# Grouped-query attention on one core: Q transposed by DMA instead of on TensorE, and separate banks for the last job's sums

## The chip, the cores and the metric

One Trainium2 chip, one core. The metric is the device time of one launch in microseconds; the median of three runs of the kernel before is 434.11 us (433.84 to 435.28).

## The reference

Grouped-query attention: 32 query heads share 8 key/value heads, so each K and V head serves four Q heads.

```python
batch, seq, n_heads, n_kv_heads, dim = 8, 512, 32, 8, 64      # Q, K, V in float32
K_expanded = np.repeat(K, heads_per_group, axis=2)            # heads_per_group = 4, same for V
scores = np.einsum('bhqd,bhkd->bhqk', Q, K_expanded) * scale  # scale = 1 / sqrt(64)
weights = np.exp(scores - np.max(scores, axis=-1, keepdims=True))
weights = weights / (np.sum(weights, axis=-1, keepdims=True) + 1e-10)
output = np.einsum('bhqk,bhkd->bhqd', weights, V_expanded)    # back to [b, q, h, d], float32
```

## The kernel before

The kernel takes exp without subtracting the row maximum (`fast_path`) and checks at the end that all row sums and the squares of V lie within bounds; a flag decides on the device whether `general_path` has to run instead. With these inputs it does not.

The work is cut into units and jobs. A unit `u` (32 of them, `NU`) is one batch and two K/V heads with their eight Q heads; `b, gp = divmod(u, 4)`. A job `j` (64, `NJOB`) is one K/V head `g` of a unit with its four Q heads, held as two pairs (`NPAIR = 2`), because two heads of 64 fill the 128 partitions. A job has 2 pairs x 4 key chunks = 8 tiles of scores, each 128 keys x (2 heads x 512 queries). TensorE computes the transposed scores (L196), so that the softmax weights come out with keys on the partitions, ready to be the stationary operand of the product with V (L262). V carries a column of ones, so the 65th column of that product is the row sum.

Seven of the eight tiles go through ScalarE: `act_tile` (L207) writes two PSUM banks, one ACTIVATE (L212) takes 128x1024 scores to f16 weights `pt`. The eighth, pair 1 and chunk 0, is computed on VectorE by bit arithmetic in three steps, `exp_d` (L220), `exp_d2` (L228, L231) and `exp_d3` (L238, L239).

The order on each engine is written out by hand in the loop at L359: `tc.manual_schedule()` keeps program order, and each engine works through its own queue with semaphores between them. Job `j`'s scores are interleaved with the weighted sums `pv(last, ...)` and the normalisation `norm(last, ...)` of the job before it, so an extra round `j = NJOB` finishes the last job. `norm` takes a reciprocal of the sums (L287), multiplies (L291) into `o_sb`, and after a unit's last pair issues the unit's store (L328) on SP's queue; the last unit is stored pair by pair. Every 16 reciprocals are checked by two instructions (`in_bounds`, L273); `check_v` (L174, L181) squares V on TensorE.

Q and K must be transposed so that the head dimension lies on the partitions. Loads cast to bf16 and are issued on POOL's queue (`load_q` L123, `load_k` L100, `load_v` L108). K of the first batch is transposed on TensorE (`first_k`); K of later batches by four DMA transposes a batch from SBUF to SBUF on SP's queue (`dma_k` L148), 128 x 512 each, and two copies (L153) that swap the halves. Q is transposed on TensorE: in job `j`, `trans_q(j + 1, ...)` makes eight transposes (L161) into one bank of `d_ps`, and VectorE copies the bank (L164) to `qt`.

PSUM has eight banks: `s_pool` 2 x 2 for ScalarE's tiles, `d_pool` 2 for VectorE's tile, the Q transposes and `check_v`, and `pv_pool` 2 for the weighted sums. `q_nat` has three buffers, so `load_q(u + 2)` at the head of job `2u` waits on POOL for the transposes of unit `u - 1`.

Of the kernel before, what the change touches and what calls it, by code (L numbers as in the profile page):

```python
# [33 lines left out]
VV_HI = 1.0e30  # L34


@with_exitstack
def kernel(
    ctx: ExitStack,
    tc: tile.TileContext,  # L40
    Q: bass.AP,
    K: bass.AP,
    V: bass.AP,
    out: bass.AP,
):
    nc = tc.nc
    flag_pool = ctx.enter_context(tc.tile_pool(name="flag", bufs=1))
    flag = flag_pool.tile([1, 1], I32, name="flag")
    with ExitStack() as fast, tc.manual_schedule():
        fast_path(fast, tc, Q, K, V, out, flag)  # L50
    good = nc.values_load(flag, min_val=0, max_val=128)
    with tc.If(good < 128):
        general_path(tc, Q, K, V, out)


def fast_path(ctx, tc, Q, K, V, out, flag):
# [11 lines left out]
    SPB = 16  # L68

    const_pool = ctx.enter_context(tc.tile_pool(name="const", bufs=1))  # L70
    qnat_pool = ctx.enter_context(tc.tile_pool(name="qnat", bufs=3))
    knat_pool = ctx.enter_context(tc.tile_pool(name="knat", bufs=2))
    qt_pool = ctx.enter_context(tc.tile_pool(name="qt", bufs=3))
    kt_pool = ctx.enter_context(tc.tile_pool(name="kt", bufs=2))
# [80 lines left out]
    def trans_q(j, bank, lo=0, hi=NPAIR):  # L155
        u, g = divmod(j, 2)
        ps = bank.bitcast(BF16).rearrange("p (i sc c) -> p i sc c", i=NPAIR, sc=SC)
        for i in range(lo, hi):
            for sc in range(SC):
                h = g * HPG + 2 * i  # L160
                nc.tensor.transpose(ps[:, i, sc, :], qn[u][:, sc, h:h + 2, :], ident)  # L161
        if j not in qt:
            qt[j] = qt_pool.tile([128, NPAIR, S], BF16, name="qt")
        return lambda: nc.vector.tensor_copy(  # L164
            out=qt[j][:, lo:hi, :], in_=ps[:, lo:hi, :, :].rearrange("p i sc c -> p i (sc c)")
        )


    def check_v(u, bank):
# [16 lines left out]

    NJOB = NU * 2
    DPAIR = NPAIR - 1
    tiles = [(i, kc) for i in range(NPAIR) for kc in range(SC) if (i, kc) != (DPAIR, 0)]
    jobs, osb, invs, ends = {}, {}, {}, []  # L190

    def scores(j, ps, i, kc, m):
# [3 lines left out]
        nc.tensor.matmul(  # L196
            ps,
            keys[64 * m:64 * m + 64, g ^ m, kc * 128:(kc + 1) * 128],
            qt[j][64 * m:64 * m + 64, i, :],
            start=True,  # L200
            stop=True,
        )

    def open_job(j):
        jobs[j] = {"pt": pt_pool.tile([128, NPAIR, SC, 2, S], FP16, name="pt")}

    def act_tile(j, n):  # L207
        i, kc = tiles[n]
        ps = s_pool.tile([128, 2, S], FP32, name="s_ps")
        for m in range(2):  # L210
            scores(j, ps[:, m, :], i, kc, m)
        nc.scalar.activation(out=jobs[j]["pt"][:, i, kc, :, :], in_=ps, func=EXP, scale=scale)  # L212

    def exp_d(j):
        st = jobs[j]
        ps = d_tile()
        for m in range(2):
            scores(j, ps[:, m, :], DPAIR, 0, m)
        st["u"] = dve_pool.tile([128, 2, S], I16, name="u16")
        nc.vector.tensor_scalar(  # L220
            out=st["u"], in0=ps, scalar1=A_U, scalar2=B_U, op0=ALU.mult, op1=ALU.add
        )

    def exp_d2(j):
        st = jobs[j]
        st["f"] = dve_pool.tile([128, 2, S], I16, name="f16")
        st["g"] = dve_pool.tile([128, 2, S], BF16, name="g16")
        nc.vector.tensor_single_scalar(  # L228
            out=st["f"], in_=st["u"], scalar=1023, op=ALU.bitwise_and
        )  # L230
# [3 lines left out]

    def exp_d3(j):
        st = jobs[j]
        w16 = dve_pool.tile([128, 2, S], BF16, name="w16")
        nc.vector.tensor_tensor(out=w16, in0=st["g"], in1=st["f"], op=ALU.mult)  # L238
        nc.vector.tensor_tensor(  # L239
            out=st["pt"][:, DPAIR, 0, :, :].bitcast(U16), in0=st["u"], in1=w16, op=ALU.add  # L240
        )

    def blocks(j):
        kcs = (1, 2, 0, 3) if j == NJOB - 1 else (1, 2, 3, 0)
        return [(kc, m, qc) for kc in kcs for m in range(2) for qc in range(SC)]

    def pv(j, i, lo, hi):
# [2 lines left out]
        b, gp = divmod(u, GP)  # L250
        if lo == 0:

            end = j == NJOB - 1 and i == NPAIR - 1
            pool, name = (s_pool, "s_ps") if end else (pv_pool, "pv")
            t = pool.tile([128, 2, S], FP32, name=name).rearrange(
                "p m (qc c) -> p m qc c", qc=SC
            )
            st["pv"] = t[:, :, :, 0:D + 1]
        order = blocks(j)
        for n in range(lo, hi):  # L260
            kc, m, qc = order[n]
            nc.tensor.matmul(  # L262
                st["pv"][:, m, qc, :],
                st["pt"][:, i, kc, m, qc * 128:(qc + 1) * 128],
                vt[b % 2][:, kc, 2 * gp + g, :],
                start=(n < 2 * SC and qc == 0),
# [3 lines left out]
    def in_bounds(outs, inv, first):  # L270
        ops = ((1.0 / SUM_HI, ALU.is_ge), (1.0 / SUM_LO, ALU.is_le))
        for out_, in1, (bound, op) in zip(outs, (first, outs[0]), ops):
            nc.vector.scalar_tensor_tensor(  # L273
                out=out_, in0=inv, scalar=bound, in1=in1, op0=op, op1=ALU.mult
            )

    def norm(j, i):
        st = jobs[j]
        u, g = divmod(j, 2)
        if u not in osb:  # L280
            osb[u] = osb_pool.tile([128, SC, 2 * HPG, D], FP32, name="o_sb")
        n = j * NPAIR + i
        k, n = divmod(n, SPB) if n < NJOB * NPAIR - 1 else (-1, 0)
        if k not in invs:
            invs[k] = inv_pool.tile([128, SPB, 2, SC], FP32, name="inv")
        inv = invs[k][:, n]
        nc.vector.reciprocal(out=inv, in_=st["pv"][:, :, :, D:D + 1])  # L287
        if k < 0:
            last_check(inv.rearrange("p m qc -> p (m qc)"))
        h = g * HPG + 2 * i  # L290
        nc.vector.tensor_tensor(  # L291
            out=osb[u][:, :, h:h + 2, :].rearrange("p qc m d -> p m qc d"),
            in0=st["pv"][:, :, :, 0:D],
            in1=inv[:, :, :, None].to_broadcast((128, 2, SC, D)),
            op=ALU.mult,
        )
# [1 line left out]
            store(u, h, h + 2)  # L298
        elif g == 1 and i == NPAIR - 1:
            store(u, 0, 2 * HPG)  # L300
        end = j == NJOB - 1 and i == NPAIR - 2
        if k >= 0 and (n == SPB - 1 or end):
            cols = (n + 1) * 2 * SC
            flat = invs.pop(k).rearrange("p s m qc -> p (s m qc)")[:, 0:cols]
            in_bounds((ok[:, 0:cols], ok[:, 0:cols]), flat, ok[:, 0:cols])
        if end:
            vmax = const_pool.tile([128, 1], FP32, name="vmax")
            nc.vector.tensor_reduce(out=vmax, in_=okv, op=ALU.max, axis=AX.X)
            okmin = const_pool.tile([128, 1], FP32, name="okmin")
# [3 lines left out]
            )  # L313


    def last_check(inv):
        cols = 2 * SC
        part = const_pool.tile([128, cols], FP32, name="part")
        right = const_pool.tile([128, cols], BF16, name="right")
        in_bounds((part, right), inv, okall[:, :].to_broadcast((128, cols)))  # L320
        count = d_tile()
        nc.tensor.matmul(count[0:1, 0, 0:cols], ones, right, start=True, stop=True)
        ends.append(count[0:1, 0, 0:cols])

# [31 lines left out]
    trans_q(0, bank[:, 0, :], 0, 1)()  # L356


    for j in range(NJOB + 1):  # L359
        real = j < NJOB  # L360
        last = j - 1
        late = last >= 0
        u, g = divmod(j, 2)
        b, gp = divmod(u, GP)
        if real:
            open_job(j)
            if j == 1:

                nc.gpsimd.tensor_copy(out=gate, in_=jobs[0]["pt"][0:1, 0, SC - 1, 0, 0:1])
                load_q(2)  # L370
            if g == 0 and u >= 1 and u + 2 < NU:
                load_q(u + 2)
            if gp == 1 and b + 1 < B:
                if g == 0:
                    load_k(b + 1)
                else:
                    load_v(b + 1)
            if gp == 2 and g == 0 and b + 1 < B:
                dma_k(b + 1)
            act_tile(j, 0)  # L380
            if j == 0:
                trans_q(0, bank[:, 1, :], 1, NPAIR)()
                act_tile(j, 1)
                exp_d(j)
            else:
                exp_d(j)
                act_tile(j, 1)
        if late:
            pv(last, 0, 0, 11)
        if real:  # L390
            act_tile(j, 2)
            exp_d2(j)
        if late:
            pv(last, 0, 11, 22)
        if real:
            act_tile(j, 3)
        if late:
            pv(last, 0, 22, 32)
            norm(last, 0)
        if real:  # L400
            act_tile(j, 4)

            bank = d_tile()
            reads = []
            if j + 1 < NJOB:
                reads.append(trans_q(j + 1, bank[:, 0, :]))
                if j == 1:
                    for swap in range(2):
                        reads.append(first_k(1, swap, bank[:, 1, swap * S // 2:]))
                elif j > 1 and b == 0 and gp + 1 < GP:  # L410
                    reads.append(first_k(gp + 1, g, bank[:, 1, :]))
            if g == 0 and u > 0:
                reads.append(check_v(u - 1, bank[:, 1, S // 2:]))
            elif j == NJOB - 1:
                reads.append(check_v(u, bank[:, 1, S // 2:]))
            for read in reads:
                read()
            exp_d3(j)
            act_tile(j, 5)
        if late:  # L420
            pv(last, 1, 0, 16)
        if real:
            act_tile(j, 6)
        if late:
            pv(last, 1, 16, 32)
            norm(last, 1)
            del jobs[last]
    nc.vector.tensor_reduce(out=flag, in_=ends[0], op=ALU.min, axis=AX.X)


# [115 lines left out]
```

## Time and profile before

| | |
|---|---|
| median of three runs | 434.11 us |
| the profiled execution, its own time | 435.11 us |
| its span, first to last instruction | 433.4 us |
| granted TensorE clock | 0.996 |
| PE / DVE / ACT busy | 388.4 / 376.7 / 414.4 us |
| first and last ACTIVATE | from 8.98 to 424.65 us |
| DMA moved | 66.97 MB in 91439 packets, mean 155 GB/s |
| q0, loads cast on the way | 25.17 MB, packets' time 49.8% of 16 engines' span |
| q1, stores, copies and transposes | 40.90 MB, 33.1% |

PE is TensorE, DVE VectorE, ACT ScalarE, POOL GpSimd, SP SyncE; SP computes nothing and issues DMAs. "L212" is line 212 of the kernel. In a row of a timeline the numbers are the start and the length of the piece in us, and the bracket at the end is the idle time before it with what ended it. In the DMA row each of 40 digits is the busy share of a slice in tenths. A share of over 1 in a window means that an engine has more than one packet under way.

### The profile page before, as it was taken

The page shows a single profiled execution, that of the slowest core. Times are in us where ns is not written, and L with a number is a line of the kernel's source. Part 1 is how long each engine was busy: PE and PEld are TensorE (multiplying, and loading weights), DVE is VectorE, ACT ScalarE, POOL GpSimd, SP SyncE. Part 2 cuts the span into 40 slices and gives each one's busy share as a digit, 9 for nine tenths or more (in the row PEclk, how much of TensorE's full clock was granted, in tenths as well). Part 3 has the DMA queues.
Part 4 walks back from the last instruction along what each step waited for, and adds up shares of the span by engine and source line. Part 5 has one row for each costly group of instructions (what it writes and reads, how often), then busy time and mean ns, then how long its engine had stood idle before and what let it go on. Part 6 is the DMA issues. An engine that isn't in the chain of part 4 may idle for free.

```text
span 433.4 us, 13542 instructions
## 1 busy us (share of the span) xinstructions
PE 388.4 (90%) x5945; PEld 243.2 (56%) x5945; DVE 376.7 (87%) x704; ACT 414.4 (96%) x449; POOL 63.9 (15%) x89
## 2 busy tenths in 40 slices
PE   7889898999989999899999999999998999999983
PEld 2455555556556556555555555555655655655552
DVE  1698998988999888998889898898899988899884
ACT  2999999999999999999999999999999999999991
POOL 8700004000040001300031000400004000000000
PEclk9999999999999999999999999999999999999998
DMA  9998756987589943998539986699757994352223
GB/s 104 178 141 181 175 151 79 217 149 190 149 128 264 144 130 120 203 210 191 144 74 208 192 192 153 78 216 154 189 149 122 264 173 108 119 146 98 98 95 106
DMA packets 91439, 66.97 MB, mean 155 GB/s; under 512 B 52080, under 2 KB 74608, under 8 KB 91376
## 3 DMA queue, kind: packets, MB, share of 16 engines
q0 software_dynamic: 56544, 25.17, 49.8%
q1 hardware_dynamic: 34832, 40.90, 33.1%
q8 instruction: 47, 0.77, 0.7%
q14 instruction: 16, 0.13, 0.2%
HBM read 50.33 MB, written 33.55 MB: 194 GB/s over the span
## 4 chain that ended last, share of the span: by engine, by line
ACT 39%; DVE 31%; PE 24%; issue 3%; POOL 1%; DVEq 0%; ACTq 0%; POOLq 0%
ACT pt L212 39%; PE s_ps L196 9%; PE pv L262 7%; DVE pt L239 7%; DVE qt L164 7%; DVE w L238 6%; PE d_ps L161 6%; DVE o_sb L291 5%; DVE inv L287 2%; DVE u L220 2%; PE d_ps L174 1%; DVE ok L273 1%; DVE f L228 1%; DVE kt_first L143 1%; POOL q_nat L123 0%
## 5 line engine op out<-in xcount | busy, mean ns | idle before, releaser
L212 ACT ACTIVATE pt<-s_ps 128x1024 f16<-128x1024 f32 x448 | 413.1, 1099 | 9.4 <-PE s_ps L196 9.0
L262 PE MATMUL pv<-v,pt 128*128 128x65 bf16 x4064 | 180.0, 195 | 18.4 <-DVE o_sb L291 18.0
L262 PEld LDWEIGHTS <-pt 128*128 128x128 f16 x4096 | 142.7, 98 | 93.7 <-issue 56.3
L196 PE MATMUL s_ps<-qt,kt 64*128 64x512 bf16 x784 | 153.5, 383 | 16.0 <-ACT pt L212 6.9
L291 DVE TENSOR_TENSOR o_sb<-pv,inv 128x512 f32<-128x512 f32 x127 | 87.8, 692 | 4.4
L196 PEld LDWEIGHTS <-kt 64*128 64x128 bf16 x896 | 54.0, 93 | 55.6 <-issue 25.0
L220 DVE TENSOR_SCALAR u<-d_ps 128x1024 int16<-128x1024 f32 x64 | 77.8, 1215 | 1.4 <-PE d_ps L196 1.4
L123 POOL DMA_DIRECT2D q_nat<-in_Q_dram x34 | 25.4, 748 | 308.0 <-PE d_ps L174 261.3
L164 DVE COPY qt<-d_ps 128x1024 bf16<-128x1024 bf16 (+1 forms) x65 | 44.4, 683 | 16.9 <-PE d_ps L174 11.7
L239 DVE TENSOR_TENSOR pt<-u,w 128x1024 uint16<-128x1024 int16 x64 | 44.3, 693 | 6.5
L238 DVE TENSOR_TENSOR w<-g,f 128x1024 bf16<-128x1024 bf16 x64 | 43.6, 682 | 0.0
L161 PE MATMUL d_ps<-ident,q_nat 128*128 128x128 bf16 x512 | 40.7, 223 | 0.9 <-DVE kt_first L143 0.9
L161 PEld LDWEIGHTS <-q_nat 128*128 128x128 bf16 x512 | 29.3, 99 | 16.2 <-issue 15.1
L287 DVE RECIPROCAL inv<-pv 128x8 f32<-128x8 f32 x127 | 25.8, 204 | 12.5 <-PE pv L262 10.9
L231 DVE TENSOR_SCALAR g<-f 128x1024 bf16<-128x1024 int16 x64 | 29.2, 457 | 2.2
L228 DVE TENSOR_SCALAR f<-u 128x1024 int16<-128x1024 int16 x64 | 27.9, 435 | 2.2
L108 POOL DMA_DIRECT2D v<-in_V_dram x32 | 28.4, 899 | 4.2 <-PE pv L262 2.5
L196 PE MATMUL s_ps<-qt,kt_first 64*128 64x512 bf16 x112 | 24.3, 431 | 1.9 <-ACT pt L212 1.1
L196 PE MATMUL d_ps<-qt,kt 64*128 64x512 bf16 x112 | 21.4, 376 | 0.0
L196 PEld LDWEIGHTS <-kt_first 64*128 64x128 bf16 x128 | 6.9, 96 | 10.3 <-issue 6.7
L174 PE MATMUL d_ps<-v 128*64 128x64 bf16 x256 | 10.6, 201 | 0.0
L174 PEld LDWEIGHTS <-v 128*64 128x64 bf16 x256 | 7.0, 110 | 3.4 <-issue 0.2
(35 smaller groups left out, 44.7 us busy)
## 6 DMA issues: line engine op xcount, KB each, us to landing
out_dram<-o_sb SPq DMA_DIRECT2D x31, 1024.0 KB, 6.2
q_nat<-in_Q_dram POOLq DMA_DIRECT2D x31, 512.0 KB, 6.3
k_nat<-in_K_dram POOLq DMA_DIRECT2D x7, 512.0 KB, 10.8
v<-in_V_dram POOLq DMA_DIRECT2D x28, 128.0 KB, 12.7
kt<-kt SPq DMA_DIRECT2D x14, 256.0 KB, 6.6
out_dram<-o_sb SPq DMA_DIRECT2D x4, 256.0 KB, 2.5
kt<-k_nat SPq DMA_TRANSPOSE x28, 4.7
v<-in_V_dram POOLq DMA_DIRECT2D x4, 96.0 KB, 8.8
```

The costliest lines, as they stand in the source:

```text
L161: nc.tensor.transpose(ps[:, i, sc, :], qn[u][:, sc, h:h + 2, :], ident)
L164: return lambda: nc.vector.tensor_copy(out=qt[j][:, lo:hi, :], in_=ps[:, lo:hi, :, :].rearrange("p i sc c -> p i (sc c)"))
L196: nc.tensor.matmul(ps, keys[64 * m:64 * m + 64, g ^ m, kc * 128:(kc + 1) * 128], qt[j][64 * m:64 * m + 64, i, :], start=True, stop=True,)
L212: nc.scalar.activation(out=jobs[j]["pt"][:, i, kc, :, :], in_=ps, func=EXP, scale=scale)
L220: nc.vector.tensor_scalar(out=st["u"], in0=ps, scalar1=A_U, scalar2=B_U, op0=ALU.mult, op1=ALU.add)
L228: nc.vector.tensor_single_scalar(out=st["f"], in_=st["u"], scalar=1023, op=ALU.bitwise_and)
L231: nc.vector.tensor_scalar(out=st["g"], in0=st["f"], scalar1=-EXP_F1, scalar2=EXP_K, op0=ALU.add, op1=ALU.mult)
L238: nc.vector.tensor_tensor(out=w16, in0=st["g"], in1=st["f"], op=ALU.mult)
L239: nc.vector.tensor_tensor(out=st["pt"][:, DPAIR, 0, :, :].bitcast(U16), in0=st["u"], in1=w16, op=ALU.add)
L262: nc.tensor.matmul(st["pv"][:, m, qc, :], st["pt"][:, i, kc, m, qc * 128:(qc + 1) * 128], vt[b % 2][:, kc, 2 * gp + g, :], start=(n < 2 * ...
L287: nc.vector.reciprocal(out=inv, in_=st["pv"][:, :, :, D:D + 1])
L291: nc.vector.tensor_tensor(out=osb[u][:, :, h:h + 2, :].rearrange("p qc m d -> p m qc d"), in0=st["pv"][:, :, :, 0:D], in1=inv[:, :, :, Non ...
```

## The change

Three edits.

First, Q of units 2 to 31 is no longer transposed on TensorE and copied by VectorE. At the head of job `2u + 1`, `dma_q(u + 2)` issues four DMA transposes on SP's queue from `q_nat` to `qt`, which now holds a whole unit (both heads). `trans_q` stays for units 0 and 1. `q_nat` has four buffers, `load_q` runs three units ahead, and `load_q(3)` is issued with `load_q(2)` in job 1.

Second, the last job's weighted sums no longer use `pv_pool`: pair 0 takes a tile of `d_pool`, pair 1 one of `s_pool`. Half of pair 0's matmuls are issued before the last job's sixth tile, the rest after the job before has been normalised; the extra round of the loop is gone. The order of the key chunks in the sums is changed (2, 3, 1, 0; in the last job 0, 1, 2, 3 and 2, 0, 1, 3).

Third, the last three reciprocals of the kernel, instead of the last one, are checked together at the end (`NLAST`), and the reductions over all earlier checks follow the fourth from last; the last unit's `check_v` moves to the last job but one. The remaining edits generalise VectorE's share of the tiles (`WIDE`, `taken`); with `WIDE` always false VectorE takes the same tile as before.

```diff
+Q_DMA_FROM = 2
+WIDE = lambda j: False
...
-    qnat_pool = ctx.enter_context(tc.tile_pool(name="qnat", bufs=3))
+    qnat_pool = ctx.enter_context(tc.tile_pool(name="qnat", bufs=4))
...
+    def dma_q(u):
+        qt[u] = qt_pool.tile([128, 2, NPAIR, S], BF16, name="qt")
+        for sc in range(SC):
+            nc.sync.dma_start_transpose(
+                out=qt[u][:, :, :, sc * 128:(sc + 1) * 128].rearrange("p g i c -> p (g i) c"),
+                in_=qn[u][:, sc, :, :].rearrange("p h d -> p (h d)"),
+            )
...
-            qt[j][64 * m:64 * m + 64, i, :],
+            qt[u][64 * m:64 * m + 64, g, i, :],
...
-    def blocks(j):
-        kcs = (1, 2, 0, 3) if j == NJOB - 1 else (1, 2, 3, 0)
+    def blocks(j, i):
+        if j == NJOB - 1:
+            kcs = (0, 1, 2, 3) if i == 0 else (2, 0, 1, 3)
+        else:
+            kcs = (2, 3, 1, 0)
...
-            end = j == NJOB - 1 and i == NPAIR - 1
-            pool, name = (s_pool, "s_ps") if end else (pv_pool, "pv")
+            if j < NJOB - 1:
+                t = pv_pool.tile([128, 2, S], FP32, name="pv")
+            else:
+                t = d_tile() if i == 0 else s_pool.tile([128, 2, S], FP32, name="s_ps")
...
+    NLAST = 3
+    inv_last = const_pool.tile([128, NLAST, 2, SC], FP32, name="inv_last")
...
+        p = j * NPAIR + i
+        left = NJOB * NPAIR - p
+        k, n = divmod(p, SPB)
+        if left <= NLAST:
+            inv = inv_last[:, NLAST - left]
...
-    for j in range(NJOB + 1):
+    for j in range(NJOB):
+        end = j == NJOB - 1
...
+            load_q(2)
+            load_q(3)
+        if g == 0 and u >= 1 and u + 3 < NU:
+            load_q(u + 3)
...
+        if g == 1 and Q_DMA_FROM <= u + 2 < NU:
+            dma_q(u + 2)
...
+        if not end:
             bank = d_tile()
...
+            if (j + 1) // 2 < Q_DMA_FROM:
                 reads.append(trans_q(j + 1, bank[:, 0, :]))
...
+            if j == NJOB - 2:
+                reads.append(check_v(u, bank[:, 1, S // 2 + D:]))
...
+        else:
+            pv(j, 0, 0, 16)
+        for read in reads:
+            read()
+        exp_d3(j)
+        act_tile(j, 5)
         if late:
             pv(last, 1, 0, 16)
...
+        if end:
+            pv(j, 0, 16, 32)
+            norm(j, 0)
+            pv(j, 1, 0, 32)
+            norm(j, 1)
```

## The prediction

> **What bounds the kernel now.** I read the page's busy times first, then ScalarE's timeline, the chain of waits at the end, the DMA row with windows of it, and SP's timeline.
>
> The page's busy line:
>
> ```profile
> PE 388.4 (90%) x5945; PEld 243.2 (56%) x5945; DVE 376.7 (87%) x704; ACT 414.4 (96%) x449; POOL 63.9 (15%) x89
> ```
>
> ACT has 448 exponentials of 413.1/448 = 0.922 us and stands at 96%. Its timeline tells where the other 4% is (third column: the idle time before the piece):
>
> ```profile
> 8.98 4.95 ACT L212 ACTIVATE pt<-s_ps 128x1024 f16<-128x1024 f32 x5 [6.81 <-PE s_ps L196]
> ...
> 46.55 29.62 ACT L212 ACTIVATE pt<-s_ps 128x1024 f16<-128x1024 f32 x32 [0.17 <-PE s_ps L196]
> 76.58 348.07 ACT L212 ACTIVATE pt<-s_ps 128x1024 f16<-128x1024 f32 x379 [0.40 <-PE s_ps L196]
> ```
>
> ACT starts at 8.98 us and, from 76.58 on, runs 379 tiles without a gap until 424.65. So nothing that PE or DVE saves between those times can shorten the program: only the 8.98 us ahead, the short waits up to 76.58 and the 8.75 us behind 424.65 are there to be won. The change leaves the number of ACT tiles as it is (`WIDE` is false everywhere). The end, from the chain that ended last:
>
> ```profile
> 424.12 0.70 DVE o_sb L291
> 424.87 1.17 PE pv L262 x32
> 426.07 0.22 DVE inv L287
> 426.31 0.69 DVE o_sb L291
> 427.00 0.20 DVE ok L273
> ...
> 428.55 0.60 DVE o_sb L291
> ```
>
> After ACT's last tile come two rounds of 32 matmuls, reciprocal and product, with the range checks between them; the last product ends at 429.15, and 4.2 us of store and shutdown follow. Beside this stands a resource that is not on the chain, the 16 DMA engines:
>
> ```profile
> DMA  9998756987589943998539986699757994352223
> ```
>
> Slices 6 to 34 of 40 average 0.70: in a batch (eight jobs, 51.4 us) the engines stand idle for some 15 us.
>
> **What goes from PE and DVE.** Jobs 4 to 63 lose 8 transposes and one copy each:
>
> ```profile
> L164 DVE COPY qt<-d_ps 128x1024 bf16<-128x1024 bf16 (+1 forms) x65 | 44.4, 683 | 16.9 <-PE d_ps L174 11.7
> L161 PE MATMUL d_ps<-ident,q_nat 128*128 128x128 bf16 x512 | 40.7, 223 | 0.9 <-DVE kt_first L143 0.9
> ```
>
> 60 x 0.683 = 41.0 us of DVE and 480/512 x 40.7 = 38.2 us of PE. Both lie beside ACT: over a batch (window 77.60 to 129.00) PE is busy 47.25 and DVE 46.45 of 51.4 us, ACT all of it. I cost their saving at nothing but ACT's waits from job 4 on, 0.17 + 0.40 = 0.57 us (bounds 0 and 0.57; the second wait comes where DVE is late with `o_sb`, and 0.68 us less per job covers it). The earlier waits stay, since jobs 1 to 3 keep their transposes. The cover is ACT; were it gone, as much as 0.6 us a job would show.
>
> **The end.** The new order gives the last job's two pairs banks of their own, so their 64 matmuls no longer wait for `o_sb`. In the times of before: the product of job 62's first pair ends at 421.95; now the range checks of that moment follow (427.00 to 428.03 before, with their first 0.08: 1.11 us), less the `check_v` reduction of 0.21; the two products of `exp_d3`, 1.48 us (422.00 to 423.48), end at about 424.4; reciprocal and product of job 62's second pair take 0.93 (425.3), of job 63's first 0.93 (426.3); the last round takes 0.24 + 0.28 (its two checks) + 0.68 = 1.20: 427.5. PE is done earlier: 423.25 after the last scores, 16 + 16 + 32 matmuls of 0.60, 0.60 and 1.17 us: 425.6. So DVE sets the end and the last product comes 1.6 us sooner (429.15 - 427.5). Bounds: 2.7, if DVE's queue did not bind (424.65 + 0.5 + 1.20 = 426.4), and 0.8, if half of it is lost to waits. The moved load of unit 3 and the four `q_nat` buffers touch nothing on this path.
>
> **What is added.** Thirty units get four DMA_TRANSPOSE each, 120, on SP's queue, each 128 x 512 into four blocks, the shape that `dma_k` already issues 28 times. SP's timeline shows its price:
>
> ```profile
> 239.09 0.37 SPq L328 DMA_DIRECT2D out_dram<-o_sb  x1
> 239.56 7.77 SPq L148 DMA_TRANSPOSE kt<-k_nat  x4
> 249.70 1.11 SPq L153 DMA_DIRECT2D kt<-kt  x2
> ```
>
> Four take SP 6.6 to 7.8 us to issue; the copy behind them, which waits for their landing, starts 8.0 to 10.1 us after the first issue (249.70 - 239.56; mean 9.1). `dma_q(u + 2)` is issued right behind store(u - 1), at the start of job 2u + 1, and is first read at job 2u + 4: three jobs, 19.3 us, so a single group leaves 10.2 us. Queued behind it on SP are the next store (12.8 us later) and, once a batch, `dma_k`. There the chain is longest: store 0.45, Q group 6.8, K group up to its copies 9.1, copies 1.1, store 0.45, Q group until landed 9.1 = 27.0 us, against five jobs, 32.1 us. SP alone is in time, by 5.1 us. On POOL the Q load now waits for the landed transposes of four units before instead of PE; K and V loads behind it have over a job to spare.
>
> What decides is the DMA engines' time. Windows cut to the packets of the seven K groups (us, then each engine's busy time, granted clock, DMA share, GB/s):
>
> ```profile
> 36.00:40.50 4.50, 3.85 (x66) 2.26 (x63) 4.26 (x9) 4.40 (x5) 0.00 (x0) 1.00 0.96 128
> 88.80:94.50 5.70, 5.13 (x80) 3.31 (x78) 4.72 (x9) 5.70 (x7) 0.00 (x0) 1.00 0.99 123
> 242.80:249.00 6.20, 5.63 (x89) 3.54 (x85) 5.19 (x11) 6.20 (x8) 0.18 (x1) 1.00 1.44 134
> 346.10:349.80 3.70, 3.23 (x50) 2.00 (x48) 3.49 (x7) 3.70 (x5) 0.00 (x0) 1.00 1.38 215
> sum 35.00, PE 31.14 PEld 19.59 DVE 30.84 ACT 34.90 POOL 0.18; mean PE 4.45 PEld 2.80 DVE 4.41 ACT 4.99 POOL 0.03
> ```
>
> A group holds the engines for 35.0/7 = 5.0 us (3.7 to 6.2) with a share of about 1 or above, though its 0.52 MB would flow in 1.8 us at the 287 GB/s that the best slices of these windows reach:
>
> ```profile
> GB/s 365 355 330 317 302 287 240 165 125 53 60 40 60 60 25 40 35 73 245 292 285 290 120 143 300 287 287 268 23 8 0 40 165 202 222 210 215 198 28 0
> ```
>
> Here, in 140.30 to 144.40, stores run out, the flow falls to 25 to 60 GB/s for 1.1 us while packets are outstanding, then comes back. I read this as transposes holding engines while they wait for a late one. No load is in flight in these windows, so whether loads could use such waits is not shown: the price of a group lies between 1.8 and 6.2 us of engine time. I take the mean, 5.0, as the only rows of this operation.
>
> The room: a batch's other work at full flow (windows where one kind runs alone: loads 202 GB/s, V 159, stores 412, copies 210) is 5 x 2.6 for Q and K, 3.3 for V, 4 x 2.55 for stores, 2.5 for copies, 5.0 for the K group: 34.0, leaving 17.4 us; the DMA row leaves 15.3. Middle: 16.3. Four Q groups ask 20.0. Each batch is short by 3.7 us; six batches have the whole load: 22.2 us, less the lead of 10.2 that must be used up first: 12.0 us of waiting, seen as ACT waiting for scores at the first jobs of a batch.
>
> The K groups move 16 blocks of 128x128 in 5.0 us. A rule of the Trainium skill speaks against the change here: VectorE: DVE Perf Modes, section The three transpose paths, gives 390 ns for such a block on TensorE and 1309 ns on the DMA crossbar, and advises TensorE where PSUM will do. Taken one after another, 16 blocks would be an estimated 20.9 us a unit, over the unit's 12.8, and the kernel some 240 us slower; the row contradicts that. Another page, DMA: Bandwidth & Descriptors, section Queues, rings and completion order, has each engine alternate between rings by packet; if that also holds while a transpose waits, loads fill the waits and the sum is that of the faster rival below.
>
> **The sum.** The profiled execution took 435.11 us, 1.7 around its span of 433.4, and lies 1.0 above the median of 434.1. Against itself: 435.1 - 1.6 - 0.6 + 12.0 = 444.9; on the scale of the median 443.9, which I give as 444. The last term is the weak one. A group at 4.4 gives 17.6 - 16.3 = 1.3 a batch, 7.8 in six, within the lead: nothing. At 6.2, 8.5 a batch: 41 us, 473.
>
> **Rivals.** Hidden (faster): If a group costs at most (16.3 + 10.2/6)/4 = 4.5 us of the engines, the lead is never used up: 434.1 - 2.2 = 431.9, with the tail's bounds 430.8 to 433.3. For it: 5.0 is close to 4.5, the two fastest groups are at 3.7 and 4.1, and part of a group's waits may serve other queues. Against: four of the seven groups take over 5.3 with nothing beside them.
>
> Used up by the waits (no change): Group 5.0, room 17.4: 2.6 short a batch, 15.6 - 10.2 = 5.4; at 4.75 it is 1.6 x 6 - 10.2, nothing. Between these, where waits pay back about 2.2 us, the time stays at 433 to 435.
>
> SP's chain late (slower): If each transpose takes SP the longest seen, 2.34 us, a group takes 9.4, and the chain 27.0 + 3 x 2.6 = 34.8 us against 32.1: 2.7 a batch, seven batches, +19: 451. It decides from 5.1 us of delay on. Against: issue is slow only behind a store that still flows.
>
> **How the numbers follow.** About 0.3%, 1.3 us, can be told from no change. Engines short (the forecast): 0.42, own range 436 to 460; SP's chain 0.08; hidden 0.40; used up 0.10. Faster 0.40, same 0.10, slower 0.50. The range takes in the hidden case from 431.0, and reaches to 460, a group of 5.6 us: (22.4 - 16.3) x 6 - 10.2 = 26.4.
>
> **What would show it.** Right: DMA row at 9 throughout, ACT waiting for PE's scores behind `qt` or `kt` DMAs at jobs 8, 16, 24, Q groups of over 4.5 us. Wrong: ACT in one piece from about 46 us on with the DMA row below 9, transposes landed well over a job ahead. The tail's step is right if the last `o_sb` comes 2.9 us after ACT's end instead of 4.5. The GB/s row at a Q group beside a load tells whether the waits are filled.

## The result and the profile after

The changed kernel takes 465.02 us (median of four runs, 461.19 to 471.34) against 434.00 before (433.84 to 435.28): ratio 1.068, 95% interval 1.0619 to 1.0741. Some runs, one of these four among them, were in a slower state, over 1.5% above the fastest run of their kernel; the ratios, and from here on all times, leave such runs out, which makes the changed kernel 463.28 us. The forecast was 444.0 with a range of 431 to 460. Slower was right, the size was not. The profiled execution of the changed kernel took 463.28 us, 1.7 around its span of 461.6; against the 435.11 of before, 28.2 us more are to be found.

The page: busy times, granted clock and DMA row.

```profile
PE 370.3 (80%) x5465; PEld 226.8 (49%) x5465; DVE 343.4 (74%) x644; ACT 416.2 (90%) x449; POOL 63.5 (14%) x89
PEclk9999999899998999999989999899999799999999
DMA  9999999999999999999899998999999999964314
```

PE has 480 instructions fewer and DVE 60, as the change says (their busy times fell by 18 and 33 us), and ACT fell from 96% to 90% of the span: it now waits. The granted clock, at 9 before in all slices but the last, dips in five slices. The DMA row, 0.70 on average in slices 6 to 34 before, is at 9 almost to the end. ACT's timeline tells where it waits (start, length, tiles, and in the bracket the idle time ahead of the piece):

```profile
8.98 4.95 ACT L236 ACTIVATE pt<-s_ps 128x1024 f16<-128x1024 f32 x5 [6.81 <-PE s_ps L218]
...
82.18 51.89 ACT L236 ACTIVATE pt<-s_ps 128x1024 f16<-128x1024 f32 x56 [2.42 <-PE s_ps L218]
138.06 3.09 ACT L236 ACTIVATE pt<-s_ps 128x1024 f16<-128x1024 f32 x3 [4.00 <-issue]
...
293.22 2.85 ACT L236 ACTIVATE pt<-s_ps 128x1024 f16<-128x1024 f32 x3 [3.13 <-issue]
...
363.83 3.09 ACT L236 ACTIVATE pt<-s_ps 128x1024 f16<-128x1024 f32 x3 [4.16 <-PE s_ps L218]
...
368.36 86.27 ACT L236 ACTIVATE pt<-s_ps 128x1024 f16<-128x1024 f32 x94 [0.18 <-PE s_ps L218]
```

What ran from 46.55 us on with a single wait of 0.40 us is cut at eleven places, each the first tile of a unit. I counted, from the end of one tile to the end of the next, what goes over ACT's pitch of 0.917 us: 34.7 us in all, against 4.7 before. Of the 30.0 more, 27.9 stand at the heads of jobs 6, 8, 10, 18, 24, 26, 32, 34, 40, 42 and 50 (0.6 to 4.3 each), 2.9 in the tiles behind them, and -0.8 before job 6. Less 1.8 us at the end (below) this makes the 28.2. After job 50 nothing waits; the last K and V loads, those of batch 7, are issued at 347 to 356 us, around that job.

What PE waited for, from the list of waits (us in total, times, longest), and from the page's table of DMA issues the median time from issue to landing:

```profile
PE s_ps L218 <- DMA qt<-q_nat: 27.8, 10, 4.2
...
PEld L218 <- DMA qt<-q_nat: 5.2, 3, 2.4
```

```profile
q_nat<-in_Q_dram POOLq DMA_DIRECT2D x31, 512.0 KB, 9.2
...
qt<-q_nat SPq DMA_TRANSPOSE x120, 8.7
...
kt<-k_nat SPq DMA_TRANSPOSE x28, 5.7
```

It is Q's transposes that come late. K's took 4.7 us to land before, and Q's loads 6.3. SP's timeline, from the store of unit 16 (job 35) to the group of unit 21:

```profile
258.48 0.38 SPq L373 DMA_DIRECT2D out_dram<-o_sb  x1
258.96 10.00 SPq L175 DMA_TRANSPOSE qt<-q_nat  x4
269.07 8.18 SPq L152 DMA_TRANSPOSE kt<-k_nat  x4
281.57 1.11 SPq L157 DMA_DIRECT2D kt<-kt  x2
282.78 0.65 SPq L373 DMA_DIRECT2D out_dram<-o_sb  x1
283.54 7.80 SPq L175 DMA_TRANSPOSE qt<-q_nat  x4
291.38 0.58 SPq L373 DMA_DIRECT2D out_dram<-o_sb  x1
292.08 8.47 SPq L175 DMA_TRANSPOSE qt<-q_nat  x4
```

This is the chain that the prediction had at 27.0 us: store, Q group, K group up to its copies, copies, store, Q group. Here the last Q transpose of unit 20 is issued at 291.34, 32.9 us after the store, with its landing still to come, and unit 20 is first read five jobs (32.1 us) after that point. ACT then waits up to 293.22, the start of job 40, the line shown above. Behind it unit 21 is late as well (job 42, 1.8 us). The same distance in each batch, with what the job that reads that group waited:

| store of unit | 0 | 4 | 8 | 12 | 16 | 20 | 24 |
|---|---|---|---|---|---|---|---|
| to the last Q issue of the unit four later, us | 32.5 | 29.9 | 29.3 | 33.3 | 32.9 | 29.4 | 27.9 |
| job that reads it, and its wait, us | 8: 2.6 | 16: 0 | 24: 1.0 | 32: 3.9 | 40: 3.2 | 48: 0 | 56: 0 |

Where the distance passes 32.1 us, the job waits; at 29.9 and below there is little or nothing. The other waits of over 1 us (10, 18, 26, 34, 42, 50) are those of the next group on the queue, the one issued behind this chain. They are the larger part: 16.6 of the 27.9 us, against 10.7 at jobs 8, 24, 32 and 40 and 0.6 at job 6. Those six groups are issued 5.1 to 9.1 us after the head of their job, because the queue is still at work on the chain, and their last transpose lands 15.6 to 17.8 us after the first issue, with the next batch's K and V loads in flight; three jobs hold 19.3 us. Units 29 to 31, issued when no load is left to fly beside them, land in 8.2 to 8.7.

Windows cut to Q groups (each engine's busy time, granted clock, DMA share, GB/s) answer the open question whether loads fill the transposes' waits; the last two show PE around the stall of job 18:

```profile
207.00:211.00 4.00, 3.47 (x54) 2.22 (x53) 3.39 (x8) 4.00 (x5) 0.00 (x0) 1.00 1.44 65
240.00:244.00 4.00, 3.53 (x61) 2.29 (x62) 3.67 (x9) 4.00 (x6) 0.97 (x2) 1.00 1.19 177
253.00:257.00 4.00, 4.00 (x55) 2.24 (x53) 2.65 (x6) 3.81 (x6) 0.00 (x0) 0.66 2.07 141
220.00:222.00 2.00, 1.84 (x32) 1.27 (x31) 1.84 (x3) 2.00 (x3) 0.00 (x0) 1.00 1.20 197
...
216.00:217.00 1.00, 0.41 (x4) 0.11 (x3) 0.97 (x3) 1.00 (x3) 0.00 (x0) 1.00 1.33 255
134.00:138.00 4.00, 0.63 (x4) 0.33 (x6) 0.31 (x1) 0.07 (x1) 0.22 (x1) 0.78 1.64 159
138.00:143.00 5.00, 5.00 (x52) 2.55 (x48) 2.99 (x6) 4.39 (x5) 0.54 (x1) 0.50 1.44 218
```

A load alone (220 to 222) flows at 197 GB/s, transposes alone (216 to 217) at 255; both in flight move 65 to 177 GB/s at a share over 1. Loads do not fill the transposes' waits: the two together move less than either alone.

The end, from the chain that ended last:

```profile
447.85 2.21 ACT pt L236 x2
...
455.25 0.69 DVE o_sb L333
456.50 0.60 DVE o_sb L333
```

ACT's last tile ends at 454.63 and the last product at 457.10, 2.5 us later (4.5 before; 2.9 forecast).

### The profile page after: what moved, and what is told of

Read it like the earlier page. It is cut to its first block, busy times and chain, and to the rows that moved or that the text cites. A ratio compares the mean times of both kernels' runs of the same rounds, so it can differ in the third digit from the quotient of the medians.

```text
span 461.6 us, 12745 instructions
## 1 busy us (share of the span) xinstructions
PE 370.3 (80%) x5465; PEld 226.8 (49%) x5465; DVE 343.4 (74%) x644; ACT 416.2 (90%) x449; POOL 63.5 (14%) x89
## 4 chain that ended last, share of the span: by engine, by line
ACT 40%; PE 20%; DMA 15%; SPq 9%; issue 2%; DVE 1%; ACTq 0%; DVEq 0%
ACT pt L236 40%; DMA qt<-q_nat 15%; PE s_ps L218 10%; PE pv L296 9%; SPq L175 9%; DVE o_sb L333 1%; PE d_ps L218 1%; PE d_ps L186 0%; ACTq L236 0%; DVE pt L265 0%; DVE w L264 0%; DVE ok L307 0%; DVE inv_last L329 0%; DVE okmin L351 0%; DVE inv L329 0%
## 5 line engine op out<-in xcount | busy, mean ns | idle before, releaser
L218 PE MATMUL s_ps<-qt,kt 64*128 64x512 bf16 x784 | 159.9, 398 | 74.4 <-ACT pt L236 32.8
L296 PEld LDWEIGHTS <-pt 128*128 128x128 f16 x4096 | 147.0, 99 | 82.4 <-issue 58.4
L296 PE MATMUL pv<-v,pt 128*128 128x65 bf16 x4032 | 183.7, 197 | 2.4 <-DVE o_sb L333 2.0
L218 PEld LDWEIGHTS <-kt 64*128 64x128 bf16 x896 | 58.7, 94 | 116.7 <-issue 79.7
L333 DVE TENSOR_TENSOR o_sb<-pv,inv 128x512 f32<-128x512 f32 x125 | 86.4, 692 | 4.5 <-DVE inv L329 0.2
L112 POOL DMA_DIRECT2D v<-in_V_dram x32 | 27.9, 885 | 30.6 <-PE pv L296 24.5
L218 PE MATMUL d_ps<-qt,kt 64*128 64x512 bf16 x112 | 22.5, 394 | 0.0
L104 POOL DMA_DIRECT2D k_nat<-in_K_dram x10 | 7.6, 765 | 1.2 <-POOLq L583 0.8
L147 DVE COPY kt_first<-d_ps 128x512 bf16<-128x512 bf16 x8 | 3.2, 418 | 5.2 <-PE d_ps L144 5.1
L193 DVE TENSOR_REDUCE okv<-d_ps 128x1 f32<-128x64 f32 x32 | 6.8, 216 | 0.0
```

Of the source, the lines that this page charges most:

```text
L112: nc.gpsimd.dma_start(out=vt[b % 2][:, sc, lo:hi, 0:D], in_=V[b, sc * 128:(sc + 1) * 128, lo:hi, :],)
L218: nc.tensor.matmul(ps, keys[64 * m:64 * m + 64, g ^ m, kc * 128:(kc + 1) * 128], qt[u][64 * m:64 * m + 64, g, i, :], start=True, stop=True,)
L296: nc.tensor.matmul(st["pv"][i][:, m, qc, :], st["pt"][:, i, kc, m, qc * 128:(qc + 1) * 128], vt[b % 2][:, kc, 2 * gp + g, :], start=(n < 2 ...
L333: nc.vector.tensor_tensor(out=osb[u][:, :, h:h + 2, :].rearrange("p qc m d -> p m qc d"), in0=sums[:, :, :, 0:D], in1=inv[:, :, :, None].t ...
```

## The experiments

Two theories went in. A (A1 and S in the later texts): the DMA engines have too little time in every batch, and lead is a credit that is used up. C (C1 and O): SP's queue, worked off in order, is longer from store to Q group than its five jobs of lead, and nothing is carried on. All kernels start from the changed one; ratios stand to the kernel before on the same chip.

### The two halves of the change

**tail_only**, no unit by DMA:

```diff
-Q_DMA_FROM = 2
+Q_DMA_FROM = 32
```

> The changed kernel with Q of every unit on TensorE again (Q_DMA_FROM = 32); the other edits stay: the last job's banks, the checks of the last three reciprocals, four q_nat buffers, Q loaded three units ahead. Theory A (the DMA engines have too little time once the Q transposes are added) and its rival C (SP's queue issues them too late) both expect the waits to be gone: 434.0 less the 1.77 us that the end of the changed kernel's profile is shorter, 432.3 us. If some other edit made the waits, about 460.

432.64 us, ratio 0.9967 [0.9954, 0.9980] to 434.28: 1.6 us. The last job's banks are worth what the prediction's end step said.

**half_units**, the odd units by DMA:

```diff
+by_dma = lambda u: u >= 2 and u % 2 == 1
...
-        if g == 1 and Q_DMA_FROM <= u + 2 < NU:
+        if g == 1 and u + 2 < NU and by_dma(u + 2):
...
-            if (j + 1) // 2 < Q_DMA_FROM:
+            if not by_dma((j + 1) // 2):
```

> Only every second unit (3, 5, 7 and so on) has its Q transposed by DMA, the others on TensorE. A: two Q groups a batch at about 4.6 us ask 9.2 of the engines' room of 14 us a batch: no waits, 432.3 us, as with all on TensorE. If a Q group cost the engines over 7 us where loads lie beside it, waits stay and it is over 434. C: SP has two groups fewer in each batch and is in time: 432.3 too.

433.37 us, 0.9984 [0.9971, 0.9997], no wait at the head of any unit. Half the transposes cost next to nothing, and win nothing either, as ACT sets the time. Which theory holds is not told by this.

### What makes it slow: bytes, transposes, or loads beside them

**plain_copies**, Q's transposes become plain copies of the same 128 KB (the blocks stay untransposed):

```diff
-            nc.sync.dma_start_transpose(
+            nc.sync.dma_start(
...
-                in_=qn[u][:, sc, :, :].rearrange("p h d -> p (h d)"),
+                in_=qn[u][:, sc, :, :].rearrange("p (k two) d -> p k (two d)", two=2),
```

> The changed kernel with each of the 120 Q transposes replaced by a plain copy of the same 128 KB from the same tile to the same tile (so the scores are of untransposed Q). If the bytes moved inside SBUF were the load, the time stays near 460. A: a copy does not hold the engines for a late one; at the 210 GB/s of the K copies a group costs 2.5 us instead of about 4.6, 8 us a batch less, and the waits go: 431 to 435. C expects the same, as SP issues a copy in 0.5 us instead of 2: this run parts bytes from the transpose as an operation, not A from C.

431.71 us, 0.9935 [0.9913, 0.9957]: two waits, 1.8 us. The same bytes on the same queue in the same order do fit; being transposes is what costs. Most of it shows in the issue: a group of copies takes SP 5.1 us on average, one of transposes 8.6, while the copies land hardly sooner (7.4 us against 8.7). The chain of the table takes 21.5 to 29.7 us here. A sentence of the Trainium skill does not hold here: Advanced Engine Details and Errata, section X-Bar Transpose (TRN2), has transposing DMAs as fast as regular ones, by which this kernel and the changed one would agree; they lie 32 us apart.

**no_q_loads**, units from 4 on use the Q of the first four units again, so Q's loads are left out:

```diff
+        if u >= 4:
+            qn[u] = qn[u % 4]
+            return
```

> The changed kernel, but Q of unit 4 and later is not loaded: the units read the first four units' Q again. All 120 Q transposes, K's and the stores stay on SP, in the same order. A: some 10 us of loads a batch leave the engines, more than the 5 us a batch that are short, so the waits go: 431 to 434 us. C: SP issues the same instructions in the same order and stays late: 450 us or more.

429.90 us, 0.990 [0.9880, 0.9919]. ACT's timeline and the DMA issues of this kernel:

```profile
139.80 282.44 ACT L239 ACTIVATE pt<-s_ps 128x1024 f16<-128x1024 f32 x308 [0.78 <-ACT pt L239]
```

```profile
qt<-q_nat SPq DMA_TRANSPOSE x120, 4.9
kt<-k_nat SPq DMA_TRANSPOSE x28, 2.6
```

All 148 transposes are there and, but for 0.78 us at job 20, nothing waits. With no Q load beside them they land in 4.9 instead of 8.7 us, K's in 2.6 instead of 5.7, the K group reaches its copies after 6.7 to 7.4 us instead of 7.4 to 14.3, and the chain of the table takes 23.9 to 26.5 us. So C in its first form, that order alone makes the chain late, falls; the chain is late because transposes beside loads are slow.

**no_v_loads**, V of batches 2 to 7 is not loaded:

```diff
     def load_v(b, lo=0, hi=KV):
+        if b >= 2:
+            return
```

> The changed kernel, but V of batch 2 and later is not loaded (the batches read the first two batches' V again). That takes 3.3 us of engine time a batch away, the smallest part of the loads. A1: about 5 us a batch are short, so a third of the 30 us of ACT's gaps stays: 438 to 446 us. C1: the V loads lie beside the Q groups of the batch's first units, not beside the K group, so the waits at a batch's second unit go (about 16 us) and those at its first stay (11): 443 to 450.

445.32 us (two runs, 443.41 and 447.23): 18 us of the 31 go with V. The two forecasts overlap there; it shows only that V's loads share in it.

**k_copies_later**, `dma_k` loses its two copies and they are issued a job later, behind the Q group:

```diff
+    def dma_k_copies(b):
...
         if g == 1 and Q_DMA_FROM <= u + 2 < NU:
             dma_q(u + 2)
+            if gp == 2 and b + 1 < B:
+                dma_k_copies(b + 1)
```

> The changed kernel with K's two half-swapping copies issued behind the next store and the next Q group instead of right behind K's transposes, so SP no longer stands until K's transposes have landed; all transfers stay. A1 (the engines' time is all used, whatever the order): the time stays at 455 to 468 us. C1 (the waits come from the in-order chain on SP - store, Q group, K group until landed, copies, store, Q group - which takes 28 to 33 us to the last issue in the changed kernel's profile against 24 to 26 without Q loads): 3 to 5 us leave the chain in each batch, most of the 27.9 us that ACT waits at the heads of units goes, 434 to 445 us.

446.24 us (two runs, 444.33 and 448.14): 9 us below A1's range, and 1 above C1's. Taking SP's wait for the K group out of the chain gives some 17 us back, with every transfer still there; what is left waits in part for the copies that now come later (PE's weight loads, 8.5 us for `kt<-kt`).

**three_of_four**, all but the first unit of a batch by DMA (`by_dma = lambda u: u >= 2 and u % 4 != 0`):

> Q by DMA for three of each batch's four units; the batch's first unit (4, 8, 12 and so on) is transposed on TensorE. A1: three Q groups at 4.4 ask 13.2 of the room of about 14 us a batch: at the edge, 432 to 438 us. C1: the last Q group leaves the chain behind the K group, and nothing is read at the batch's first job but K's copies: 432 to 435.

451.21 us (two runs, 449.91 and 452.51). A1 missed by 13 us and C1 by 16. GpSimd's timeline shows what is different:

```profile
232.66 0.74 POOL L127 DMA_DIRECT2D q_nat<-in_Q_dram  x1 [17.76 <-DMA qt<-q_nat]
233.39 0.75 POOL L104 DMA_DIRECT2D k_nat<-in_K_dram  x1
234.27 3.48 POOL L112 DMA_DIRECT2D v<-in_V_dram  x4
237.73 0.77 POOL L127 DMA_DIRECT2D q_nat<-in_Q_dram  x1
```

The second of these Q loads reuses the buffer of the batch's second unit, whose transposes have landed by 232.1 here, as no group of the first unit is queued ahead of them. So two Q loads, K and V go out in one row within 6 us, and SP's timeline has Q groups, issued while such loads are in flight, that take twice the 6.8 us of the prediction:

```profile
193.84 14.14 SPq L175 DMA_TRANSPOSE qt<-q_nat  x4
...
248.08 13.98 SPq L175 DMA_TRANSPOSE qt<-q_nat  x4
```

Fewer transposes in a batch, and still 17 us slower than before: their number alone does not tell the time, and what flies beside them counts.

**v_late**, V's load moved from job 8b + 1 to the middle of job 8b + 6, held back by a one-element copy on GpSimd:

```diff
...
-            else:
-                load_v(b + 1)
...
         act_tile(j, 3)
+        if gp == 3 and g == 0 and b + 1 < B:
+            nc.gpsimd.tensor_copy(out=gate, in_=jobs[j]["pt"][0:1, 0, SC - 1, 0, 0:1])
+            load_v(b + 1)
```

> V of the next batch is loaded at the middle of job 8b + 6 instead of at job 8b + 1, where it lies beside Q's transposes; a one-element copy on GpSimd holds it back until then. Bytes and transposes are the same. If only the sum of the engines' time counts (A1): unchanged, 460 to 468. If loads and transposes in flight together are what costs (theory L), part of what leaving V out gave (448.9): 448 to 458. Should V meet the next group in its new place, nothing is won and L is not told from A1 by this.

470.25 us (465.81 to 470.71), 1.0871 [1.0815, 1.0926]. V met the next Q group in its new place (groups of 11.12 and 13.80 us), and the copy holds up the Q load behind it. Inconclusive, as the expectation allowed for.

### Is lead a credit that is used up?

**more_lead**, transposes and loads of Q one unit earlier:

```diff
-    qnat_pool = ... bufs=4
+    qnat_pool = ... bufs=5
-    qt_pool = ... bufs=3
+    qt_pool = ... bufs=4
...
             load_q(3)
-        if g == 0 and u >= 1 and u + 3 < NU:
-            load_q(u + 3)
+            load_q(4)
+            dma_q(2)
+        if g == 0 and u >= 1 and u + 4 < NU:
+            load_q(u + 4)
...
-        if g == 1 and Q_DMA_FROM <= u + 2 < NU:
-            dma_q(u + 2)
+        if g == 1 and u + 3 < NU:
+            dma_q(u + 3)
```

> A change that leaves the bytes and the order of the groups as they are: each Q unit's transposes are issued one unit (12.8 us) earlier, its load too, with one more qt and one more q_nat buffer. If the DMA engines simply have too little time in each batch (theory A1), lead is a credit that is spent once: 465.0 - 12.8 = 452 (448 to 456), the waits starting later but as long per batch from then on. If the order on SP's queue is too long only around the K group (theory C1: store to the fourth group after it 28 to 35 us, against 32.1 us of five jobs), seven jobs (44.9 us) are enough for it and nothing waits: 432 to 437, ACT in one piece.

445.06 us, 1.0248 [1.0227, 1.0268]: between the two. Its ACT timeline, a row of its waits, its DMA row, and windows of three batches in it:

```profile
74.71 3.10 ACT L236 ACTIVATE pt<-s_ps 128x1024 f16<-128x1024 f32 x3 [10.78 <-PE s_ps L218]
...
186.14 253.23 ACT L236 ACTIVATE pt<-s_ps 128x1024 f16<-128x1024 f32 x276 [0.18 <-PE s_ps L218]
```

```profile
PEld L218 <- DMA kt<-kt: 14.0, 3, 10.2
```

```profile
DMA  9999999999999999999999999999999995885214
```

```profile
200.00:251.40 51.40, 43.65 (x681) 27.50 (x677) 41.78 (x79) 51.40 (x58) 8.13 (x10) 1.00 1.26 221
251.40:302.80 51.40, 43.72 (x678) 27.49 (x674) 42.03 (x79) 51.40 (x58) 7.22 (x9) 1.00 1.33 206
302.80:354.20 51.40, 43.79 (x678) 27.44 (x674) 42.10 (x78) 51.40 (x57) 7.24 (x9) 1.00 1.30 203
```

This is the run that decides. Three whole batches, with all their loads, stores and at least 20 transposes each, go by in 51.4 us each while ACT is busy in all of it (51.40). The DMA row is at 9, and yet nothing is short. Nor is lead being eaten: from the last Q issue of the first unit of a batch to the end of the job ahead of its first use it is 21.4, 21.7, 21.2 and 18.5 us in batches 4 to 7; with 3.7 us short a batch it would have fallen by 11. What is left, 1.1 us at job 4, 10.9 at job 8 and some 4 us at jobs 13 to 24, is the start: SP issues two Q groups together at 21 us, and the first K group comes so late that its copies are waited for (`DMA kt<-kt`).

**lead_from4**, the same with units 2 and 3 left on TensorE, so that the start has no such backlog:

```diff
-Q_DMA_FROM = 2
+Q_DMA_FROM = 4
```

> As more_lead, but units 2 and 3 keep their transposes on TensorE, so that the first K group isn't queued behind twelve Q transposes. Theory S (every batch asks more of the DMA engines than 51.4 us hold; lead is a credit): 23 us of lead against 3.7 to 5 us a batch in six batches leaves 0 to 7 us of waits in the last batches, and the distance between a group's issue and its first use shrinks from batch to batch: 433 to 440. Theory O (SP's chain around the K group is longer than its five jobs of lead, and nothing is carried on to the next batch): no waits, a distance that doesn't shrink, 432 to 434. What tells them apart is the trend of the distance more than the time.

441.32 us (438.92 to 442.76), 1.0139 [1.0095, 1.0183]. Lists of waits and ACT's timeline:

```profile
PEld L218 <- DMA kt<-kt: 10.8, 3, 7.7
```

```profile
121.81 3.09 ACT L236 ACTIVATE pt<-s_ps 128x1024 f16<-128x1024 f32 x3 [7.65 <-PE s_ps L218]
...
279.71 154.54 ACT L236 ACTIVATE pt<-s_ps 128x1024 f16<-128x1024 f32 x168 [1.80 <-PE s_ps L218]
```

The trend, which was to tell the two apart, speaks for O: Q's distance is 15.0, 19.3, 18.1, 17.5, 20.4 and 19.5 us in batches 2 to 7 and does not shrink. Neither time is met: S's 433 to 440 is missed by 1 us, O's 432 to 434 by 7. Three waits are left (jobs 16, 32, 40; 10.5 us), none for Q. They are for K's copies, whose four jobs of lead are now the shortest on the queue: they were waited for where the last K transpose was issued 5.7, 11.7 and 10.7 us ahead of the batch, and not at 13.2 and more. A version with the K group earlier as well was not measured, so that this would end the waits is argued, not shown.

**v_late_lead**, both edits:

> Both edits: V's load at the middle of job 8b + 6, and Q's transposes and loads one unit earlier. A1: 452 as more_lead alone. L: the lower of the two less what V gives, 435 to 446. C1: 432 to 437.

461.89 us (459.90 to 462.51), 1.0616 [1.0581, 1.0651], all three theories missed. More lead without the gate gives 445; the gate costs 17 us here and 7 us in v_late. A load that is held back comes out in a bunch with the next ones, as in three_of_four; that this bunch is the whole 17 us is not shown.

### Can the freed time be used?

**half_wide**, half_units and, in 15 even jobs, a third half tile of exponentials for VectorE:

```diff
-WIDE = lambda j: False
+WIDE = lambda j: j >= 6 and j % 4 == 2
```

> Every second unit's Q by DMA, as in the run half_units, and in the first job of each such unit VectorE takes three half tiles instead of two, so ACT has one 128x512 less in 15 of 64 jobs. If DVE has the room that the missing copies leave (0.69 us in each job ahead of a unit by DMA; a third half tile costs about 1.75 us of DVE in two jobs), ACT saves about 0.4 us in each of 15 jobs: 433.4 - 6 = 427 us. If DVE becomes late, ACT waits and the gain is lost: 433 or more.

428.96 us, 0.988 [0.9853, 0.9906]: the fastest of all that compute the whole reference, 5 us below before. ScalarE's 15 half tiles (0.70 us each instead of 0.92 for a whole one) are the gain, in two pieces without a wait:

```profile
45.45 182.02 ACT L236 ACTIVATE pt<-s_ps 128x1024 f16<-128x1024 f32 x200 [0.17 <-PE s_ps L218]
227.78 191.65 ACT L236 ACTIVATE pt<-s_ps 128x1024 f16<-128x1024 f32 x211 [0.32 <-PE s_ps L218]
```

**half_wider**, seven more such jobs (`j >= 6 and (j % 4 == 2 or j % 8 == 3)`):

> Odd units' Q by DMA as in half_wide, and seven more jobs (the second job of every fourth unit, 11, 19 and so on) give a third half tile of exponentials to VectorE. ScalarE sets the time of half_wide (429.0); fifteen wide jobs were worth 432.6 - 429.0 = 3.7 us, 0.25 each, so seven more give 1.7: 427.2. If VectorE, 377 us busy of 427 in half_wide, gets too full in those jobs: 429 to 432.

433.28 us, 0.9979 [0.9963, 0.9995]: just over the second forecast. PE waits 26.6 us, 48 times, for DVE's `o_sb` before it may overwrite the sums (13.8 us, 38 times, in half_wide). VectorE is busy 387.0 of 433.4 us and has become the engine that others wait for.

**lead_wide**, lead_from4 and 27 wide even jobs (`j >= 10 and j % 2 == 0`):

> As lead_from4, and the even jobs from 10 on (27) give a third half tile of exponentials to VectorE, whose queue lost Q's copies. Fifteen such jobs were worth 3.7 us (432.6 - 429.0), 0.25 each: 27 are worth 6.7, and VectorE has 27 x 1.14 = 31 us more to do, about 378 of 427 us. If nothing waits for a DMA: 426 to 427.5. If S is right: 430 to 440.

441.48 us, 1.0153 [1.0115, 1.0192], no better than lead_from4. ScalarE has 6.7 us less to do, and waits for K's copies at jobs 16, 32, 40 and 48 instead of three: with shorter jobs, four of them are a shorter lead (argued from the list of waits, not tested).

## Why the prediction was wrong, point by point

**PE and DVE relief at nothing: right.** half_units takes half of the transposes off both engines and gains nothing over tail_only.

**The end, 1.6 us: right.** tail_only measures 1.6; in the changed kernel it is 1.8.

**SP's chain, 27.0 us, "in time, by 5.1 us": wrong, and the first step that failed.** Its terms were durations of before, where no load flew beside a transpose in those windows. A transpose takes SP 2.1 us on average (up to 4.75), so a Q group 8.6 instead of 6.8; K group to copies 7.4 to 14.3, mean 11.5, instead of 9.1. With these the chain is 0.5 + 8.6 + 11.5 + 1.2 + 0.6 + 8.6 = 31.0 us to the last issue, on average, with the landing still to come, against 32.1: no margin is left, and three of seven batches are over. That is the rival "SP's chain late", which had 34.8 us, 2.7 a batch, 451, and a chance of 0.08. What spoke against it, "issue is slow only behind a store that still flows", was read from a profile that could not show the other case. The second price of that step fell with it: a single group, 9.1 us to its landing against three jobs of 19.3, was to leave 10.2 us; the six groups read at jobs 10, 18, 26, 34, 42 and 50 started 5.1 to 9.1 us late behind the chain and landed 15.6 to 17.8 us after their first issue.

**The engines' time, "each batch is short by 3.7 us": wrong as a cause.** The price of a group beside loads was rightly seen to be unknown, and 4 x 5.0 of 16.3 us of room came out near the edge. But more_lead does the same work in 51.4 us a batch without a wait, and its distance does not shrink. The row at 9 throughout, which the prediction named as its proof, is there in the waitless batches too, so it proves nothing. Single transfers take longer, but a batch's transfers still fit into its 51.4 us.

**"Less the lead of 10.2": wrong with it.** Lead was taken as a store that a deficit empties once. It is what a chain has to fit into, anew in every batch: no batch carries its lateness on, and of the seven behind the first only the last is spared. The first 10.2 us of lateness were not free: jobs 6, 8 and 10 already wait 5.8 us. In the measured terms: 435.1 - 1.8 - 0.8 + 27.9 + 2.9 = 463.3, where 12.0 stood for the last two.

**Signs.** ACT waiting behind `qt` at the heads of units: right; "at jobs 8, 16, 24": only 8 and 24, and more often one unit later (six waits against four), which the prediction did not think of: once unit 4b is transposed, GpSimd's queue lets out Q, K and V loads together, beside the group of unit 4b + 1.

**PE's restart, not foreseen:** 2.9 us. In 134 to 138 of the windows PE does next to nothing and its clock falls to 0.78, in the 5 us behind it is 0.50; the three ACT tiles behind the wait of 4.00 take 1.03 us each, paced by PE. Shorter waits had it too: windows right behind those of 1.62 (252.4 to 255.7) and 3.13 us (293.3 to 296.7, where the tiles take 0.95) show 0.50, while the 3.4 us behind the wait of 1.72 (from 307.8) show 1.00. Page TensorE: Matmul & The Clock Gate of the Trainium skill, section Part 1: The HAM clock gate, puts the limit at an idle window of about 3.4 us and the rate behind it at half. The rate fits; the limit does not, as PE had stood for only 1.9 us ahead of the first of these windows.

What stays open is why a transpose is slow beside a load. That it is, no_q_loads shows (a Q transpose lands in 4.9 instead of 8.7 us). The other direction is weaker: Q's loads land in 9.2 us beside the transposes, 8.4 beside plain copies, 6.3 before. Whether packets that alternate, a shared port, or the load's cast is behind it, no run tells; nor why SP takes longer to issue a transpose than a copy.

## What to carry to other kernels

An in-order queue has to be priced by its longest chain between two deadlines, with the durations it will have beside the new traffic, not those of a quiet profile; some 0.4 us on each of twelve issues was the whole margin. Before a busy share is called a shortage, give the transfers one more buffer of lead: if the waits leave and the lead stays, it was latency. And where relieving one engine wins nothing, look for work that it can take from the engine that sets the time: half of the change with 15 half tiles moved to VectorE beat both kernels.

## What the runs showed of the hardware that was not expected

- Transposes (SBUF to SBUF, 128 KB each) and casting loads from HBM in flight together: 65 to 177 GB/s at a DMA share of 1.2 to 2.1; each alone 255 and 197.
- Issuing one of Q's DMA transposes takes SP 1.2 to 4.75 us in the changed kernel, 2.1 on average, and 1.9 with Q's loads left out; its landing 8.7 and 4.9 us.
- A DMA row of 9 in every slice is no proof of a full resource: batches at a share of 1.26 to 1.33 went by without one wait of ScalarE, at 203 to 221 GB/s.
- TensorE's granted clock stood at 0.50 for the 5 us behind an idle time of 4.0 us, and for some 3.4 us behind idle times as short as 1.8 us (window 183.6 to 187.0 of more_lead), though not behind every one of that length.
